# Hybrid GLA/MLA decoder layer on one core: the place of a head's block totals, and the order of accumulating transfers behind them

## The chip, the cores and the metric

The kernel runs on one core of a Trainium2 chip. The metric is the device time of one execution in microseconds; the time before is the median of three runs, 871.81 us (871.01 to 873.06). The engines have short names: PE (TensorE, with PEld for its weight loads), DVE (VectorE), ACT (ScalarE), POOL (GpSimd) and SP (SyncE). Each engine works through its own queue in order. Transfers are issued from the queue of an engine; in this kernel those that add into their destination are issued from POOL.

## The reference, cut to what matters

One layer on 512 tokens of width 1024, in float32. The normalised input goes through one wide input projection `w_in`, whose columns are split among a gated linear attention (GLA, four heads with 128 key and 256 value channels), a latent attention (MLA, eight heads) and two gates. Both branches are projected, gated, added and projected again; a squared-ReLU MLP follows. The part around the change is the GLA, for each head:

```
h = layer_norm(x);  q, k, v, r, a_lr, ... = split(h @ w_in)
log_a = log_sigmoid(a_lr @ w_gla_a2 + b_gla_a2) / 16
o_i = sum over j <= i of  (q_i * k_j * exp(sum of log_a over j+1..i)) . v_j
o   = rms_norm(o) * silu(r),  then @ w_o_gla
```

## The kernel before, in words

**The large products.** `w_in` is read in column sections. Each section r, v, a and b (the GLA's r and v, and the two gates) is one call of `unit`: a 512x1024x1024 product by a Winograd-like scheme with seven products n = 0 to 6 instead of eight. Their right sides are `RPH = ("T1","11","22","T2","21","T3","T4")`. "11", "22" and "21" are quarters of the section. T1, T2, T3 and T4 are sums of quarters, and they are made by transfers: `r_load` loads a quarter, and `r_add` adds another quarter into the tile that is there, by a transfer from POOL with `accum_op=add` (L623). T1 is loaded by SP (L625) and added into ahead of its unit, in `r_begin`. T2 is T1 with another quarter added, T3 is "22" with one added, and T4 is T2 with one added, each in two halves. An add must wait until the tile's old content has been used (split, below) or loaded.

**Splits.** Each right side is split into a high part (ACT, L190) and the remainder (DVE, L191), as the products run in three passes (L791 to L793 and L797 to L799) on such parts. `pump` traces the splits a little ahead of their use.

**GLA levels.** `gla_levels(h)` makes the scores of head h within a 512-token sequence by levels s = 1, 2, 4, ..., 256: at level s, pairs of neighbouring blocks of s tokens are multiplied. For each level ACT packs the operands into M (`pack`, L902), PE multiplies (L937), DVE takes the block into the scores (L909) and lets the decay in k grow to the next level (`grow`, L884), for which it needs the decay of whole blocks. These block totals come from `totals(h)`: seven additions on POOL, each of half the length of the last (L859, from 256 elements to 4), then two exponentials on ACT, of the head's log decays (L862) and of the totals (L863). `products(h)` makes q times k for the diagonal on POOL (L867), its high part on ACT (L869) and the remainder on POOL (L870). For head 0 both are traced when its levels begin (L917), for every other head in the fifth level (s = 16) of the head in front of it (L931).

**Order of the work.** The levels of all heads are one generator, `lane_levels`; `unit` advances it, with others, by `tick`: after each of its products but the last, and in unit r also in the middle of products 0, 2, 4 and 6, in the later units in the middle of each. So in unit r the levels of head 0 are traced like this: s = 1 behind product 0, s = 2 behind product 1, s = 4 in the middle of product 2, s = 8 behind it, s = 16 behind product 3. `r_add` for T2 is traced in product 0, that for T3 in product 2, the one for T4 in product 3, and that for the T1 of the next unit (`r_begin`) in product 3 too.

What is traced is not yet what is queued. The tile framework plans the queues (`schedule_with_timeline_sim=True`): what is traced earlier has priority, but whatever its own model of the time holds ready goes first. `tc.issue_after(ins)` adds an edge of order alone: what the block traces on the engine of `ins` is queued behind `ins`, without a wait for its end. On the chip each engine then keeps to the queue that was planned.

Of the kernel before, what the change touches and what calls it, by code (L numbers as in the profile page):

```python
# [16 lines left out]
ALU = mybir.AluOpType  # L17
# [9 lines left out]
GH = 4  # L27
# [25 lines left out]
def tile_hybrid_block(ctx: ExitStack, tc: tile.TileContext, I, out, dbg=None):  # L53
# [19 lines left out]
    def A(shape, dt=F32, n="a"):  # L73
        tag, bufs = ("C", 8) if n in TAG_C else (n, TAG_W[n]) if n in TAG_W else ("A", 24)
        return pa.tile(shape, dt, tag=tag, bufs=bufs, name=nm(n))

    def B(shape, dt=F32, n="b"):
        return pb.tile(shape, dt, tag="B", name=nm(n))
# [11 lines left out]
    def PX(shape=(P, T), dt=F32, n="px"):  # L90
        return px.tile(list(shape), dt, tag="px", name=nm(n))

    def f(ap):
        return ap.bitcast(F32)
# [5 lines left out]
    gtt = nc.gpsimd.tensor_tensor  # L100
# [8 lines left out]
    def split(src, hi, lo, scale=None):  # L109
        if scale is None:  # L110
            act(hi, src, AF.Copy)
            return vtt(lo, src, f(hi), op=ALU.subtract)
        else:
            act(hi, src, AF.Copy, scale=scale)
            return stt(lo, src, scale, f(hi), op0=ALU.mult, op1=ALU.subtract)
# [29 lines left out]
    st = {"dma": 0, "spl": 0, "gates": ()}  # L145
# [470 lines left out]
    def r_load(sec, op, i, j, hf, add=False):  # L616
        w = I["w_in"].rearrange("(k p) n -> p k n", p=P)
        if not add:
            RW[sec, op, hf] = A([P, 2, T], F32, "rw")
        k0 = 4 * i + 2 * hf  # L620
        c0 = UCOL[sec] + j * T
        if add:
            nc.gpsimd.dma_start(RW[sec, op, hf], w[:, k0:k0 + 2, c0:c0 + T], accum_op=ALU.add)  # L623
        else:
            nc.sync.dma_start(RW[sec, op, hf], w[:, k0:k0 + 2, c0:c0 + T])  # L625

    def r_begin(sec):
        for hf in range(2):
            r_load(sec, "T1", 0, 1, hf)
        r_add(sec, "T1", "T1", 0, 0)  # L630

    def r_add(sec, dst, src, i, j):
        for hf in range(2):
            RW[sec, dst, hf] = RW[sec, src, hf]
            r_load(sec, dst, i, j, hf, add=True)

    KEPT = {}

# [72 lines left out]
    def unit(sec, nxt=None):  # L711
# [65 lines left out]
        for n in range(7):  # L777
            o = a if n in (1, 3, 5) else b
            for hf in range(2):
# [22 lines left out]
                if n == 0 and hf == 1:  # L802
                    r_add(sec, "T2", "T1", 1, 1)
                    if later:
                        fetch("S2")
                if n == 2 and hf == 1:
                    r_add(sec, "T3", "22", 0, 1)
                    if later:
                        fetch("S3")
# [39 lines left out]
    QKP = [None] * GH  # L849
# [3 lines left out]
    def totals(h):  # L853
        t = TOT[h] = B([P, T], F32, "tot")
        src, o, n = GL[h], 0, T // 2
        while n >= 4:
            a = src.rearrange("p (n two) -> p n two", two=2)
            src = t[:, o:o + n]
            gtt(src, a[:, :, 0], a[:, :, 1], op=ALU.add)  # L859
            o += n  # L860
            n //= 2
        act(GL[h], GL[h], AF.Exp, scale=1.0 / 16.0)  # L862
        act(t[:, :o], t[:, :o], AF.Exp, scale=1.0 / 16.0)  # L863

    def products(h, qk):
        pr = B([P, T], F32, "pr")
        gtt(pr, qk[:, 0, :], qk[:, 1, :], op=ALU.mult)  # L867
        QKP[h] = [B([P, T], F32R, "qkp") for _ in range(2)]
        act(QKP[h][0], pr, AF.Copy)  # L869
        gtt(QKP[h][1], pr, f(QKP[h][0]), op=ALU.subtract)  # L870

    def gla_levels(h):
        qk = QK[h]
        QK[h] = None
        SD = B([P, NT, P], F32, "SD")
        s128 = kq = None

        def view(t, off, side, blk, step, s):
            return bass.AP(tensor=t.tensor, offset=t.offset + off, ap=[t.ap[0], [side, 2], [blk, T // (2 * s)], [step, s]])

        def grow(s):
            new = view(qk[:, 0, :], 0, T + s, 2 * s, 1, s)
            tot, o = (GL[h], 0) if s == 1 else (TOT[h], T - 2 * T // s)
            vtt(new, new, view(tot, o + 1, -1, 2, 0, s), op=ALU.mult)  # L884

        def half_lr(t2, s, i):
            v = t2[:, 0, :]
            return bass.AP(tensor=v.tensor, offset=v.offset + 2 * i * P,
                           ap=[v.ap[0], [2 * s, P // s], [T + s, 2], [1, s]])

        def packed(M, s, i):
            v = M[:, i, 0, :]
            return bass.AP(tensor=v.tensor, offset=v.offset,
                           ap=[v.ap[0], [2 * s, P // s], [s + (-2 * P if i else 2 * P), 2], [1, s]])

        def taken(v, s, step):
            return bass.AP(tensor=v.tensor, offset=v.offset + s, ap=[v.ap[0], [step, 2], [2 * s, P // s], [1, s]])

        def pack(s):
            M = B([P, 2, 2, P], F32, "M")  # L900
            for i in range(2):
                act(packed(M, s, i), half_lr(qk, s, i), AF.Copy)  # L902
            return M

        def take(s, p):
            nonlocal s128, kq
            if s <= 64:
                mk = lmask[:, LEVELS.index(s)].rearrange("p o u (n s) -> p o (u n) s", s=s)
                nc.vector.copy_predicated(taken(SD[:, 0, :], s, 2 * P - s), mk, taken(p[:, :2 * P], s, -s))  # L909
            elif s == 128:  # L910
                s128 = B([P, 2, 2, P], F32R, "s128")
                split(p[:, :256].rearrange("p (a b) -> p a b", b=P), s128[:, 0], s128[:, 1])
            else:
                split(p[:, :256], kq[:, 0, 0], kq[:, 0, 1])


        if h == 0:  # L917
            totals(0)
            products(0, qk)
        vtt(qk[:, 1, :], qk[:, 1, :], GL[h], op=ALU.mult)  # L920
        s = 1
        M = pack(1)
        yield
        diag = PX()
        for w in range(2):
            mm(diag, ones, QKP[h][w], start=w == 0, stop=w == 1)
        prev = None
        while s < T:
            if s == 2:
                vtt(SD, diag.rearrange("p (t i) -> p t i", i=P), ident[:, None, :].to_broadcast([P, NT, P]), op=ALU.mult)  # L930
            if s == 16 and h + 1 < GH:  # L931
                totals(h + 1)
                products(h + 1, QK[h + 1])
            p = PX()
            if s <= 64:
                for u in range(2):
                    mm(p[:, u * P:(u + 1) * P], M[:, 0, u, :], M[:, 1, u, :], start=True, stop=True)  # L937
            elif s == 128:
                for i in range(2):
                    mm(p[:, i * P:(i + 1) * P], qk[:, 0, 2 * i * P:(2 * i + 1) * P],  # L940
                       qk[:, 1, (2 * i + 1) * P:(2 * i + 2) * P], start=True, stop=True)
            else:
                for j in range(2):
                    nc.tensor.transpose(p[:, j * P:(j + 1) * P], qk[:, 0, j * P:(j + 1) * P], ident)
                kq = A([P, 2, 2, 256], F32R, "kq")
                split(qk[:, 1, 256:], kq[:, 1, 0], kq[:, 1, 1])
            if prev is not None:
                take(*prev)
            prev = (s, p)
            if s < 256:  # L950
                grow(s)
            s *= 2
            if s <= 64:
                M = pack(s)
            yield
        sd = A([P, 2, NT, P], F32R, "sd")
        p = PX()
        for u in range(2):
            nc.tensor.transpose(p[:, u * P:(u + 1) * P], SD[:, 2 + u, :], ident)
        act(sd[:, 0, :2], SD[:, :2], AF.Copy)  # L960
        gtt(sd[:, 1, :2], SD[:, :2], f(sd[:, 0, :2]), op=ALU.subtract)
        take(*prev)
        yield
        pt = p[:, :2 * P].rearrange("p (u i) -> p u i", i=P)
        split(pt, sd[:, 0, 2:], sd[:, 1, 2:])
        SS[h] = (sd, s128, kq)
        if h != 2:
            yield
# [212 lines left out]
    def lane_levels():  # L1181
        for o in range(2):
            with tc.issue_after(last_in.ins):
                nc.vector.tensor_copy(lmask[:, :, o], lmi[:, o, :, None, :].to_broadcast([P, len(LEVELS), 2, 64]))
        for h in range(GH):
            yield from gla_levels(h)
            lv[h] = True
# [413 lines left out]
```

## Time and profile before

| what | value |
|---|---|
| median of three runs | 871.81 us (871.01 to 873.06) |
| the profiled execution's own time | 871.12 us |
| its span, first to last instruction | 869.3 us |
| PE busy | 850.9 us, 98% of the span |
| DVE, ACT, POOL busy | 630.1, 485.7, 189.4 us |
| mean granted TensorE clock | 0.995 |
| L623, adds into tiles of sections | 32, 39.7 us of POOL |

The prediction works against the profiled execution, as all durations are its own, and then moves to the median. Rows of a timeline read: start in us from the span's start, duration in us, engine, line, operation, output and inputs by the program's names, shapes, count; in brackets how long the engine stood idle in front of it, and what ended that. In a table of waits a row reads: who waits, for whom, microseconds in total, times, the longest. In a table of groups: line, engine, operation, names and shapes, count, busy microseconds, mean nanoseconds of one, idle time in front. Rows that begin with a stretch of time give for each engine its busy time in it, with the number of instructions, then the granted clock, the DMA share and the rate.

### The profile page before, as it was taken

The numbers are of one execution on the slowest core, as the hardware profiler recorded it, in microseconds if no ns is written. First come the engines' busy times: TensorE is split into PE (matmuls) and PEld (weight loads), VectorE is DVE, ScalarE is ACT, GpSimd is POOL, SyncE is SP. The second block draws the span as 40 slices with busy tenths as digits, with TensorE's granted clock in tenths as the row PEclk, the third lists the DMA queues.
The fourth block names the chain that finished last, engine by engine and source line by source line (L and its number), as shares of the span: only waits on it lengthen the run. The fifth ranks groups of instructions, "written<-read, shape, count | busy, mean of one in ns | idle before, by whom it ended". The sixth has DMA issues, their size and how long they took to land. (4 is left out here: it accounts for less than half of the span.)

```text
span 869.3 us, 12408 instructions
## 1 busy us (share of the span) xinstructions
PE 850.9 (98%) x4594; PEld 736.0 (85%) x4594; DVE 630.1 (72%) x1023; ACT 485.7 (56%) x830; POOL 189.4 (22%) x220
## 2 busy tenths in 40 slices
PE   8999998999999999999999999999999999999995
PEld 5988777889999989888888888988888888888884
DVE  7967978988776657567766888986567546854687
ACT  5367757757674635455555324485366446745662
POOL 2304651625222210000000021005301520331023
PEclk9999999999999999999999999999999999999998
DMA  7746899998997614123136355008922990497075
GB/s 239 220 122 225 238 294 258 296 312 219 292 252 178 206 35 125 31 55 104 49 142 215 129 156 209 1 1 252 260 69 49 290 220 23 86 315 180 1 193 97
DMA packets 80924, 144.19 MB, mean 166 GB/s; under 512 B 9153, under 2 KB 35188, under 8 KB 80864
## 3 DMA queue, kind: packets, MB, share of 16 engines
q1 hardware_dynamic: 56480, 87.63, 29.8%
q0 software_dynamic: 22464, 52.11, 27.9%
q10 hardware_dynamic: 1920, 3.66, 1.3%
q8 instruction: 36, 0.59, 0.3%
q14 instruction: 24, 0.20, 0.1%
HBM read 116.64 MB, written 12.58 MB: 149 GB/s over the span
## 5 line engine op out<-in xcount | busy, mean ns | idle before, releaser
L191 DVE TENSOR_TENSOR wlo<-wraw,whi 128x1024 fp32r<-128x1024 f32 (+3 forms) x82 | 91.6, 1118 | 91.3 <-ACT whi L190 91.0
L190 ACT ACTIVATE whi<-wraw 128x1024 fp32r<-128x1024 f32 (+3 forms) x82 | 78.6, 959 | 62.7 <-PE mm L242 31.7
L242 PE MATMUL mm<-h,whi 128*128 128x512 f32 x288 | 112.1, 389 | 0.0
L241 PE MATMUL mm<-h,whi 128*128 128x512 f32 x288 | 112.1, 390 | 0.0
L243 PE MATMUL mm<-h,wlo 128*128 128x512 f32 x288 | 107.2, 389 | 0.0
L1463 POOL DMA_DIRECT2D res<-ev x54 | 47.7, 995 | 237.9 <-ACT ev L1461 194.3
L623 POOL DMA_DIRECT2D rw<-in_w_in_dram x32 | 39.7, 1240 | 110.4 <-DVE wlo L191 43.0
L243 PEld LDWEIGHTS mm<-h,wlo 128*128 128x128 f32 x288 | 54.0, 188 | 11.3
L241 PEld LDWEIGHTS mm<-h,whi 128*128 128x128 f32 x288 | 54.1, 188 | 11.1
L242 PEld LDWEIGHTS mm<-h,whi 128*128 128x128 f32 x288 | 54.1, 188 | 11.1
L191 DVE TENSOR_TENSOR wlo<-rw,whi 128x1024 fp32r<-128x1024 f32 x32 | 40.7, 1271 | 16.0 <-ACT whi L190 15.7
L1528 ACT ACTIVATE relu<-mm 128x512 f32<-128x512 f32 x32 | 18.8, 595 | 57.2 <-PE mm L243 57.2
L190 ACT ACTIVATE whi<-rw 128x1024 fp32r<-128x1024 f32 x32 | 33.8, 1057 | 18.7 <-PE mm L792 10.3
L382 POOL TENSOR_TENSOR mv<-mv,mhalf 128x1 f32<-128x1 f32 x4 | 4.1, 1035 | 169.3 <-DVE mv L381 169.3
L190 ACT ACTIVATE xh<-wraw 128x1024 fp32r<-128x1024 f32 (+1 forms) x24 | 23.3, 979 | 26.5 <-PE mm L276 15.2
L791 PE MATMUL mm<-S,whi 128*128 128x256 f32 x128 | 36.3, 288 | 0.0
L792 PE MATMUL mm<-S,whi 128*128 128x256 f32 x128 | 35.7, 283 | 0.0
L793 PE MATMUL mm<-S,wlo 128*128 128x256 f32 x128 | 34.5, 285 | 0.0
L191 DVE TENSOR_TENSOR wlo<-wq,whi 128x1024 fp32r<-128x1024 f32 x15 | 18.3, 1223 | 20.4 <-ACT whi L190 20.4
L191 DVE TENSOR_TENSOR xl<-wraw,xh 128x1024 fp32r<-128x1024 f32 (+1 forms) x24 | 26.2, 1110 | 5.9 <-ACT xh L190 5.9
L902 ACT ACTIVATE M<-qk 128x256 f32<-128x256 f32 x56 | 23.9, 456 | 8.4 <-DVE qk L884 7.5
L1461 ACT ACTIVATE ev<-mm 128x512 f32<-128x512 f32 x20 | 11.9, 601 | 27.8 <-DMA res<-ev 19.3
(473 smaller groups left out, 2730.4 us busy)
## 6 DMA issues: line engine op xcount, KB each, us to landing
rw<-in_w_in_dram POOLq DMA_DIRECT2D x32, 512.0 KB, 8.0
wraw<-in_w_ff_dram SPq DMA_DIRECT2D x32, 512.0 KB, 8.1
wq<-in_w_ff_dram POOLq DMA_DIRECT2D x32, 512.0 KB, 9.7
res<-ev POOLq DMA_DIRECT2D x54, 256.0 KB, 8.4
wraw<-in_w_in_dram SPq DMA_DIRECT2D x24, 512.0 KB, 5.0
S<-S SPq DMA_DIRECT2D x24, 512.0 KB, 6.7
rw<-in_w_in_dram SPq DMA_DIRECT2D x16, 512.0 KB, 8.7
S<-s SPq DMA_DIRECT2D x8, 512.0 KB, 5.1
```

The costliest lines, as they stand in the source:

```text
L190: st["ins"] = act(hi[:, :nk, :n], raw[:, :nk, :n], AF.Copy)
L191: vtt(lo[:, :nk, :n], raw[:, :nk, :n], f(hi[:, :nk, :n]), op=ALU.subtract)
L241: mm(o, hi[:, c], xh, start=first, stop=False)
L242: mm(o, hi[:, c], xl, start=False, stop=False)
L243: mm(o, lo[:, c], xh, start=False, stop=last)
L623: nc.gpsimd.dma_start(RW[sec, op, hf], w[:, k0:k0 + 2, c0:c0 + T], accum_op=ALU.add)
L791: mm(d, hi[:, c], xh, start=opens and q % 2 == 0, stop=False, skip_group_check=True)
L792: mm(d, hi[:, c], xl, start=False, stop=False, skip_group_check=True)
L793: mm(d, lo[:, c], xh, start=False, stop=closes, skip_group_check=True)
L902: act(packed(M, s, i), half_lr(qk, s, i), AF.Copy)
L1463: nc.gpsimd.dma_start(res[tt + t][:, j * T:(j + 1) * T], e, accum_op=ALU.add)
L1528: act(r, ps, AF.Relu)
```

## The change

The totals and products of head h + 1 are traced in the second level (s = 2) of head h, not in the fifth (s = 16). The last instruction of `products`, the subtraction on POOL, is remembered; every accumulating transfer that `r_add` traces after it has an edge of order to it, so that it stands behind the most recent `products` in POOL's queue. In unit r the adds into T2 are traced after products of head 0, and the adds into T3, into the T1 of unit v and into T4 are now traced after those of head 1.

```diff
@@ r_add
         for hf in range(2):
             RW[sec, dst, hf] = RW[sec, src, hf]
-            r_load(sec, dst, i, j, hf, add=True)
+            with ExitStack() as behind:
+                if "pool" in st:
+                    behind.enter_context(tc.issue_after(st["pool"].ins))
+                r_load(sec, dst, i, j, hf, add=True)
@@ products
-        gtt(QKP[h][1], pr, f(QKP[h][0]), op=ALU.subtract)
+        st["pool"] = gtt(QKP[h][1], pr, f(QKP[h][0]), op=ALU.subtract)
@@ gla_levels
-            if s == 16 and h + 1 < GH:
+            if s == 2 and h + 1 < GH:
                 totals(h + 1)
                 products(h + 1, QK[h + 1])
```

## The prediction

> **What bounds the kernel now.** I read the head of the page first, then the table of who waited for whom with TensorE alone, then the timelines of PE, ACT and POOL around its longest entry.
>
> ```profile
> span 869.3 us, 12408 instructions
> ...
> PE 850.9 (98%) x4594; PEld 736.0 (85%) x4594; DVE 630.1 (72%) x1023; ACT 485.7 (56%) x830; POOL 189.4 (22%) x220
> ...
> PE px L937 <- ACT M L902: 3.2, 1, 3.2
> ```
>
> TensorE is busy for 98% of the span, so the end of the kernel moves only when TensorE works with fewer holes. The last line is the head of the table of its waits (who waits, for whom, microseconds in total, times, longest): its longest single wait in the whole span is 3.2 us, once, for the packed operand M of a GLA level. The timeline of PE shows where, and what it costs beyond the hole itself (start, duration, engine, line, operation).
>
> ```profile
> 126.19 0.60 PE L937 MATMUL px<-M 128*128 128x128 f32 x4
> ...
> 126.87 0.40 PE L797 MATMUL mm<-whi,s 128*128 128x512 f32 x1
> 127.10 0.39 PE L798 MATMUL mm<-wlo,s 128*128 128x512 f32 x1
> ...
> 129.15 0.39 PE L797 MATMUL mm<-whi,s 128*128 128x512 f32 x1
> 132.69 1.02 PE L937 MATMUL px<-M 128*128 128x128 f32 x4 [3.16 <-ACT M L902]
> ...
> 133.93 0.63 PE L799 MATMUL mm<-whi,s 128*128 128x512 f32 x1
> ...
> 136.44 0.40 PE L797 MATMUL mm<-xh,s 128*128 128x512 f32 x1
> ```
>
> Before the hole one 512-column matmul follows another at 0.23 us (126.87 to 127.10). The next one after 129.15 was due at 129.38 and came at 132.69: 3.31 us lost. Behind it a matmul takes 0.63 us instead of 0.39: the six from 133.93 to 136.44 took 2.51 us where six at 0.23 are 1.38, so 1.13 are lost, and of the 1.24 us from 132.69 to 133.93 the same ratio (2.51 to 1.38) loses 0.56. The slow clock costs 1.7 us, and the hole 5.0 us together. The next two timelines show its cause.
>
> ```profile
> 119.54 0.64 ACT L869 ACTIVATE qkp<-pr 128x512 fp32r<-128x512 f32 x1
> 120.06 1.07 ACT L190 ACTIVATE whi<-rw 128x1024 fp32r<-128x1024 f32 x1
> ...
> 121.96 0.73 ACT L902 ACTIVATE M<-qk 128x256 f32<-128x256 f32 x2
> 130.46 0.63 ACT L863 ACTIVATE tot<-tot 128x508 f32<-128x508 f32 x1 [7.77 <-POOL tot L859]
> ...
> 131.94 0.70 ACT L902 ACTIVATE M<-qk 128x256 f32<-128x256 f32 x2
> ```
>
> ACT stands 7.77 us for the block totals of head 1, which only head 1's levels need, much later. ACT works its queue in order, so a weight split and the M of 131.94 stand behind it, and TensorE behind that M.
>
> ```profile
> 89.06 1.24 POOL L623 DMA_DIRECT2D rw<-in_w_in_dram  x1 [8.37 <-DVE xl L191]
> ...
> 97.53 1.34 POOL L870 TENSOR_TENSOR qkp<-pr,qkp 128x512 fp32r<-128x512 f32 x1
> ...
> 105.08 1.23 POOL L623 DMA_DIRECT2D rw<-in_w_in_dram  x1
> 105.86 0.78 POOL L584 MEMSET krl<- 128x256 f32 x1
> ...
> 112.23 1.16 POOL L859 TENSOR_TENSOR tot<-g 128x256 f32<-128x256 f32 x1
> 113.35 1.73 POOL L867 TENSOR_TENSOR pr<-qk 128x512 f32<-128x512 f32 x1
> ...
> 124.93 1.20 POOL L623 DMA_DIRECT2D rw<-in_w_in_dram  x1 [5.29 <-DMA rw<-in_w_in_dram]
> ...
> 128.42 1.20 POOL L623 DMA_DIRECT2D rw<-in_w_in_dram  x1 [0.78 <-DMA rw<-in_w_in_dram]
> 129.19 1.23 POOL L859 TENSOR_TENSOR tot<-tot 128x16 f32<-128x16 f32 x3
> ```
>
> POOL started head 1's totals at 112.23 and ended them at 130.42, because accumulating transfers lie between them in its queue. Those of 124.93 and 128.42 waited for the plain load into the same tile: they are the two adds into T1 of unit v, the only ones here whose tile a plain load fills. The other adds, in the order of their tiles, are T2 of unit r (89.06 and one more), T3 (105.08 and one more) and T4.
>
> **The change, part by part.** Walking the ticks of unit r: the second level of head 0 is traced behind product 1, the fifth behind product 3. So totals(1) and products(1) move two products forward: ahead of the adds of T3, of v's T1 and of T4, which were all traced ahead of them.
>
> *The stall.* The v T1 adds now have an edge behind the last products instruction, and the totals, traced ahead of that, come first by priority. Their waits for loads until 124.9 and 128.3 then hold nobody: what POOL has next is the split of head 0's scores, at the end of its levels. Removed: 5.0 us.
>
> *The moved instructions.* They are the same ones, with no more DMAs; one head's share is a quarter of these rows:
>
> ```profile
> L859 POOL TENSOR_TENSOR tot<-tot 128x128 f32<-128x128 f32 (+5 forms) x24 | 16.6, 693 | 0.7
> L867 POOL TENSOR_TENSOR pr<-qk 128x512 f32<-128x512 f32 x4 | 7.1, 1779 | 0.0
> L870 POOL TENSOR_TENSOR qkp<-pr,qkp 128x512 fp32r<-128x512 f32 x4 | 6.5, 1616 | 0.0
> L859 POOL TENSOR_TENSOR tot<-g 128x256 f32<-128x256 f32 x4 | 6.4, 1594 | 0.0
> ...
> rw<-in_w_in_dram POOLq DMA_DIRECT2D x32, 512.0 KB, 8.0
> ...
> rw<-in_w_in_dram POOLq DMA_DIRECT2D x1, 512.0 KB, 10.2
> ```
>
> That is (16.6 + 7.1 + 6.5 + 6.4) / 4 = 9.2 us of POOL for a head. The last two rows are the time from issue to landing of an add, the median of all and the one issued between 111 and 115 us. The memset of 105.86 is traced ahead of the totals, so I let head 1's work begin at 106.6, in time in which POOL now only waits.
>
> *What is late next.* v T1's second add, 128.42 + 8.0, lands at 136.4. Without the hole TensorE comes to it after products 5 and 6 (24 matmuls each, 5.5 us) and half of product 0, at 126.87 + 11.0 + 2.8 = 140.7; its split takes 2.3 us, so 2.0 are left (at 10.2 us it is 0.2 late). I take nothing off.
>
> *T2 of unit r.* Its adds now stand behind products(0), whose last instruction ends at 97.53 + 1.34 = 98.9. The first moves from 89.06 to 98.9, ten us, and the second stays 1.2 us behind it. The first lands at 98.9 + 8.0 = 106.9, or 109.1 with 10.2 us.
>
> ```profile
> 107.48 1.08 ACT L190 ACTIVATE whi<-rw 128x1024 fp32r<-128x1024 f32 x1
> ...
> 114.12 0.39 PE L797 MATMUL mm<-whi,s 128*128 128x512 f32 x1
> ```
>
> ACT splits it at 107.48 and TensorE uses it at 114.12; the split takes 1.08 us on ACT and 1.2 on DVE (the row of 107.93 below), so even at 109.1 it is ready near 111.4. Cost 0; the cover is the 2.7 us that are left.
>
> *T3 of unit r.* From 106.6 the last products instruction ends between 112.0 (first totals, product, ACT's copy and the remainder, about 5.4 us) and 115.8 (all 9.2 us first). So the first T3 add goes from 105.08 to 112.0–115.8, and the second 1.2 behind it. It lands between 120.0 (8.0) and 126.0 (10.2). TensorE needs its low part at 127.10; less 1.2 on DVE and 1.07 on ACT, ACT must start by 124.7; now it starts at 120.06. At the near end it costs nothing. At the far end ACT stands until 126.0, and the M behind both splits, now done at 122.7, would be done near 128.9 for the level that TensorE has at 126.19: 2.7 us. In the middle (landing 122 to 123) it is covered, and I take 0.5.
>
> *DVE beside POOL.* The moved work now runs beside a full DVE:
>
> ```profile
> 105.00:110.00 5.00, 5.00 (x24) 4.13 (x22) 5.00 (x8) 5.00 (x10) 1.97 (x4) 1.00 0.72 160
> ...
> 107.93 1.21 DVE L191 TENSOR_TENSOR xl<-rw,xh 128x1024 fp32r<-128x1024 f32 x1
> ...
> 111.10 0.68 DVE L884 TENSOR_TENSOR qk<-qk,tot 128x512 f32<-128x512 f32 x1
> 113.05 0.88 DVE L884 TENSOR_TENSOR qk<-qk,tot 128x512 f32<-128x512 f32 x1
> ...
> 159.81 2.35 DVE L884 TENSOR_TENSOR qk<-qk,tot 128x512 f32<-128x512 f32 x1
> 163.59 2.63 DVE L191 TENSOR_TENSOR wlo<-wraw,whi 128x1024 fp32r<-128x1024 f32 x1
> ...
> 110.68 0.39 PE L798 MATMUL mm<-xl,s 128*128 128x512 f32 x1
> ```
>
> The first row is the table of windows (PE, PEld, DVE, ACT, POOL busy): DVE and ACT are busy for all 5 us. Beside head 1's totals the product of L884 took 0.88 for 0.68 alone; beside head 2's it took 2.35, and a split 2.63 for 1.21. So one head stretches DVE by between 0.2 and (1.67 + 1.42) = 3.1 us. The split of 107.93 ends at 109.14 and is used at 110.68, 1.5 us of cover: TensorE pays 0 to 1.6 us. Head 1's row is the same product of the same unit, so I stay near it: 0.5. From below: DVE at 112 to 117 is relieved of the same, which is worth nothing as TensorE doesn't wait there.
>
> The Trainium skill speaks against this place: "GPSIMD Engine Reference", section 8, says that GpSimd shares its SBUF interfaces with VectorE and contends with VectorE instructions that have two SBUF inputs. The trace bears it out unevenly, 0.88 and 2.35 us for the same instruction; by the rule alone the larger stretch would be taken, 1.6 instead of 0.5, and the sum would be −2.9.
>
> *Heads 2 and 3.* Their totals move two products forward in the units v and a. TensorE waits for nothing there now, so nothing is won, and adds behind them may come up to one head's 9.2 us later: I take 0, with up to 1 us either way in the range.
>
> Sum: −5.0 + 0.5 + 0.5 = −4.0 us. The profiled execution took 871.12 us (its span and 1.8 around it), which gives 867.1. The median of the three runs is 0.69 above it: **867.8 us**. What a measurement can tell from no change is about 0.2%, 1.74 us.
>
> **The rivals.** *Stretched DVE (gain given back).* The splits of 107.93 and three more two-input instructions until 112 each take 1.4 to 1.7 us longer, as beside head 2: about 6 us, less 1.5 of cover. TensorE waits 4.5 and the time is 871.3, no change. For it: DVE is full there and cannot catch up. Against it: 0.88 at 113.05. With smaller T3 delays added the same band is reached; together 0.17. This is also where the skill's rule on the shared interfaces would lead.
>
> *Head 1's copy stays late (slower).* The adds of T3 hang on the copy of the products on ACT, L869. In the trace that copy ran at 119.54, though its product was ready at 113.35 + 1.73 = 115.1: ACT, in order, had other work. If ACT, which is full from 105 to 110, gets to it no sooner than now, products(1) end at 120.2 + 1.6 = 121.8, the first T3 add lands at 129.8 to 132.0, and its low part is ready at 132.1 to 134.3 against 127.1. TensorE then stands 5.0 to 7.2 us, with about 1.7 for the clock: 6.7 to 8.9 instead of 5.0, so 873.5 to 875.7, middle 874.6. It decides from an issue of T3 near 117 on (landing past 125 to 127); slower than before it is from about 120. For it: the copy was 4.5 us late in the trace. Against it: it is now traced ahead of T2's split, so it comes ahead of it by priority. Chance 0.15.
>
> On a short wait the Trainium skill ("TensorE: Matmul & The Clock Gate", Part 1) has the array throttled only after an idle window of about 3.4 us. By that rule a rest of 2.7 us mostly keeps its clock; no row here shows a hole of that size.
>
> *It doesn't do what it says.* The edge binds the adds to the products only, and not to the small totals, which have waits of their own; an add that the planner thinks ready could slip between them again and ACT would stand as before: 871.8. Against it: the adds whose loads come late are now two products behind. Chance 0.05.
>
> **How the numbers follow.** The forecast (gain between 1.8 and 5.5 us) has 0.61, the stretched DVE with small delays 0.17, the unchanged wait 0.05, slower 0.16 with all other mishaps, other small changes 0.01. That gives faster 0.61, same 0.23, slower 0.16. The range begins at the whole gain with half a microsecond from heads 2 and 3 and the spread of the runs below their median (0.8): 871.8 − 5.0 − 1.3 = 865.5. It ends where the slower case begins, 873.5. The likeliest case alone has 866.3 to 870.0.
>
> **What would show it.** Right: in the timeline of ACT no wait for the totals between 120 and 131, in that of PE no hole at 129 to 133 and 0.23 us pitches through it; POOL's totals of head 1 in one piece before 116, and the two v T1 adds behind them. The T2 adds of unit r start near 99. DVE's instructions at 107 to 112 stay near 0.9 and 1.3 us. Wrong: TensorE waiting for a low part (L191) or an M between 108 and 130, a T3 add issued later than 117, or a granted clock under 1.00 in a new place.

## The result, and the profile after

The changed kernel takes 877.1 us (median of 20 runs, 875.65 to 880.35); the kernel before, on the same chip, 871.2 us (20 runs). The ratio is 1.0067, 95% interval 1.0055 to 1.0080: by the ratio slower by 5.8 us, where 4.0 less were forecast. The profiled execution took 876.68 us.

The head of its page (the span, then busy time by engine):

```profile
span 874.6 us, 12402 instructions
...
PE 852.9 (98%) x4594; PEld 736.9 (84%) x4594; DVE 629.7 (72%) x1023; ACT 486.1 (56%) x830; POOL 191.1 (22%) x220
```

The span is 5.3 us longer, 2.0 of it busy time on TensorE (matmuls that take longer under a slow clock, below) and the rest idle. Two timelines of PE show where. First the kernel before, at the end of unit r, at both halves of the first product of unit v, and at the first matmul of the latent attention's queries:

```profile
143.74 0.38 PE L944 MATMUL px<-ca,qk 128*128 128x128 f32 x2
...
145.00 0.71 PE L797 MATMUL mm<-whi,S 128*128 128x512 f32 x2
...
147.82 0.39 PE L797 MATMUL mm<-xh,S 128*128 128x512 f32 x1
...
292.11 0.40 PE L274 MATMUL mm<-whi,latT 128*128 128x256 f32 x2
```

Then the changed kernel (its lines stand three further down):

```profile
140.17 0.38 PE L947 MATMUL px<-ca,qk 128*128 128x128 f32 x2
140.39 0.38 PE L962 MATMUL px<-ca,SD 128*128 128x128 f32 x2
140.53 0.71 PE L929 MATMUL px<-qkp,ones 128*128 128x512 f32 x2
144.47 1.22 PE L940 MATMUL px<-M 128*128 128x128 f32 x4 [3.23 <-ACT M L905]
145.35 1.20 PE L800 MATMUL mm<-whi,S 128*128 128x512 f32 x2
...
147.50 0.63 PE L802 MATMUL mm<-whi,S 128*128 128x512 f32 x1
147.93 0.63 PE L801 MATMUL mm<-wlo,S 128*128 128x512 f32 x1
...
151.29 0.39 PE L800 MATMUL mm<-xh,S 128*128 128x512 f32 x1
...
297.54 0.40 PE L274 MATMUL mm<-whi,latT 128*128 128x256 f32 x2
```

At the end of unit r the change is 3.6 us ahead (140.17 against 143.74). The second half of unit v's first product starts 3.5 us behind (151.29 against 147.82): 7.0 us are lost between. There is a new hole of 3.23 us, and behind it matmuls 0.43 us apart instead of 0.23 until 150.92 (granted clock 0.50 from 145 to 151). By the query product another 2.0 are lost (5.4 behind), and this stays to the end (5.3). Unit v has no part in these 2.0: unit a starts at 191.49 against 188.00, still 3.5 behind. Behind that start TensorE waits twice for a low part (0.97 us at 200.91, 0.58 at 244.51; in the kernel before once, 0.3). The first of these low parts is late for two reasons. ACT stood 2.85 us for T1 of unit a until 193.24, and VectorE behind it; then two VectorE subtractions take 1.86 us each instead of 0.68, while POOL runs head 3's first sum and product from 196.61 (the timelines of DVE and, last, of PE):

```profile
195.81 3.72 DVE L112 TENSOR_TENSOR vl<-rg,vh 128x512 fp32r<-128x512 f32 x2
199.44 1.41 DVE L191 TENSOR_TENSOR wlo<-wraw,whi 128x1024 fp32r<-128x1024 f32 x1
...
200.91 0.38 PE L796 MATMUL mm<-h,wlo 128*128 128x256 f32 x1 [0.97 <-DVE wlo L191]
```

The timeline of ACT says who made the hole of 3.23 us:

```profile
111.77 0.63 ACT L866 ACTIVATE tot<-tot 128x508 f32<-128x508 f32 x1 [2.47 <-POOL tot L862]
...
142.81 1.06 ACT L190 ACTIVATE xh<-rw 128x1024 fp32r<-128x1024 f32 x1 [4.97 <-DMA rw<-in_w_in_dram]
143.77 0.65 ACT L905 ACTIVATE M<-qk 128x256 f32<-128x256 f32 x1
144.22 1.05 ACT L190 ACTIVATE whi<-rw 128x1024 fp32r<-128x1024 f32 x1
```

The wait of 7.77 us for head 1's totals has become one of 2.47, at 111, and no long hole of TensorE follows it. The new one, 4.97 us, is for the second half of unit v's T1. Behind that split ACT's queue holds the M that TensorE waits for, and then the split of the first half. POOL's timeline shows that the change does what it says:

```profile
97.49 2.47 POOL L623 DMA_DIRECT2D rw<-in_w_in_dram  x2
...
104.72 0.61 POOL L862 TENSOR_TENSOR tot<-g 128x256 f32<-128x256 f32 x1
...
107.53 4.21 POOL L862 TENSOR_TENSOR tot<-tot 128x128 f32<-128x128 f32 x6
111.69 1.74 POOL L873 TENSOR_TENSOR qkp<-pr,qkp 128x512 fp32r<-128x512 f32 x1
113.38 3.65 POOL L623 DMA_DIRECT2D rw<-in_w_in_dram  x3
...
127.11 1.20 POOL L623 DMA_DIRECT2D rw<-in_w_in_dram  x1 [6.35 <-DMA rw<-in_w_in_dram]
131.09 1.20 POOL L623 DMA_DIRECT2D rw<-in_w_in_dram  x1 [2.78 <-DMA rw<-in_w_in_dram]
```

Head 1's totals run in one piece from 104.72 to 111.7; T2's adds leave at 97.49, and T3's with the first of T4 at 113.38. But the two adds into v's T1 wait for their plain loads until 127.11 and 131.09, against 124.93 and 128.42 before, and the second lands at 142.7. SP issued these loads 1.7 and 1.4 us later than before (from 115.52 on, against 113.81), and the second of them took 14.5 us to land instead of 13.1.

### The profile page after: what moved, and what is told of

Read it like the earlier page. It is cut to its first block, busy times and chain, and to the rows that moved or that the text cites. A ratio compares the mean times of both kernels' runs of the same rounds, so it can differ in the third digit from the quotient of the medians.

```text
span 874.6 us, 12402 instructions
## 1 busy us (share of the span) xinstructions
PE 852.9 (98%) x4594; PEld 736.9 (84%) x4594; DVE 629.7 (72%) x1023; ACT 486.1 (56%) x830; POOL 191.1 (22%) x220
## 5 line engine op out<-in xcount | busy, mean ns | idle before, releaser
L796 PE MATMUL mm<-h,wlo 128*128 128x256 f32 x96 | 25.9, 285 | 1.6 <-DVE wlo L191 1.6
```

Source lines behind the costliest of these rows:

```text
L796: mm(d, lo[:, c], xh, start=False, stop=closes, skip_group_check=True)
```

## The experiments

**Theory A**: the edge holds T3's adds behind head 1's products, so that they join the transfers that already crowd the time from 113 on; v's T1 lands later and ACT stands for it. **Its rivals**: the moved POOL work itself costs (B), the adds and totals still block each other (C), the loss lies with the later heads (D, E, F below). Ratios are to the kernel before on the same chip, with 95% intervals. Diffs are against the changed kernel unless said.

**No edge at all.** The four lines of `ExitStack` and edge are taken out; the totals stay at s = 2.

> Totals and products in the second level, no edge on any accumulating transfer. Theory A (the edge pushes the two T3 adds of unit r from 105-110 us to 113.4 us, into the busiest time of the transfers, so that the T1 adds of unit v land at 142.7 and not at 138, and ACT stands for them): T3 adds back at 105-110, v's second T1 add lands by 139.5, ACT waits under 1 us for it, the hole of TensorE at 141-144 is gone and the one of 129-132 stays away; 866 to 869 us where before has 871, ratio 0.994 to 0.998. Theory B (the moved POOL work itself, beside DVE and ahead of ACT's queue, delays the splits, and the edge has little to do with it): the hole at 141 stays, 874 to 877 us, ratio 1.004 to 1.007. Theory C (the two adds that wait for loads get between the totals again): the hole of 129 is back, 871.

872.92 us, ratio 1.0028 (1.0017 to 1.0038). That lies in none of the expected bands: the edge makes more than half of the loss, and not all of it.

**The edge alone.**

```diff
-            if s == 2 and h + 1 < GH:
+            if s == 16 and h + 1 < GH:
```

> Totals and products in the fifth level as before, the edges kept: only the T2 adds of unit r are later (behind the products of head 0, 97 us), and the totals of head 1 still have adds between them. Theory A: T2 late costs nothing; the hole at 129-132 stays, none at 141; ratio 0.999 to 1.002. If late T2 adds were what hurts: ratio over 1.004, with ACT or TensorE waiting for T2 between 107 and 115 us.

870.42 us, ratio 0.9997 (0.9984 to 1.0009). With the totals at the old place the edge costs nothing, though T2's adds leave late in it, too. So the edge costs only together with early totals.

**The edge, but not on T3.**

```diff
-                if "pool" in st:
+                if "pool" in st and dst != "T3":
```

> As after the change, but with the adds into T3 alone free of the edge (T2, T1 and T4 keep it). Theory A: the T3 adds go back to 105-110 us, which is enough: no hole at 141, 866 to 869 us, ratio 0.994 to 0.998, the same within 1 us as without any edge. Theory B: still 874 to 877, ratio 1.004 to 1.007.

872.81 us, ratio 1.0028 (1.0015 to 1.0041): the same as with no edge. What the edge costs is its hold on T3.

**The totals at s = 8**, behind product 2, where T3's adds are already traced.

> Totals and products in the fourth level (s = 8), traced behind the T3 adds and ahead of the T1 adds of the next unit; edges as after the change. Theory A: T3 adds free at 105-110, totals of head 1 before v's T1 adds: neither hole; 865 to 868 us, ratio 0.993 to 0.997. Theory B (POOL work beside a full DVE is what hurts): also better than after, since the work goes back to about 110-118 us, ratio 0.996 to 1.000. This run tells little between A and B alone; it is the version that either would choose.

871.89 us, ratio 1.0017 (1.0006 to 1.0028). T3 is not held here (its adds leave at 103.90 and 108.50), but those of T4 are, and still there is no gain: in its profiled execution, the fastest of this kernel (868.74), ACT stands 4.50 us for T4 at 130.25 and 3.70 us for v's T1 at 138.43.

**T3 of unit r cut to a quarter.** The two transfers carry 128 of their 512 columns.

```diff
-            nc.gpsimd.dma_start(RW[sec, op, hf], w[:, k0:k0 + 2, c0:c0 + T], accum_op=ALU.add)
+            n = T // 4 if (sec, op) == ("r", "T3") else T
+            nc.gpsimd.dma_start(RW[sec, op, hf][:, :, :n], w[:, k0:k0 + 2, c0:c0 + n], accum_op=ALU.add)
```

> As after the change, in the same queue places, but the two T3 adds of unit r move a quarter of their columns (128 of 512; three quarters of that sum are left out, so the output is another). Theory A2 (the T3 adds hurt by their bytes: pushed to 113.4 us, they share the transfer engines with the plain loads into v's T1, which then land late): those loads land 1 to 3 us sooner than at 127.1 and 131.0, v's second T1 add lands under 141, ACT's wait for it falls from 5.0 to 3 or less, and product 0 of unit v reaches its second half before 149 us instead of at 151.3; ratio 1.002 to 1.005. Rival (only the queue place counts: POOL or SP stands in order, and ACT's 2.5 us wait for head 1's totals delays SP): nothing moves, second half of product 0 at 151 +- 0.7, ratio 1.006 to 1.008.

872.71 us, ratio 1.0021 (1.0011 to 1.0031). That looks like proof that those bytes, coming late, delay T1. It is none: the control at the end of this section shows that the same cut helps the kernel before by as much.

**Head 1 alone at s = 2, no edge on T3.** Heads 2 and 3 go back to s = 16.

```diff
-                if "pool" in st:
+                if "pool" in st and dst != "T3":
...
-            if s == 2 and h + 1 < GH:
+            if s == (2 if h == 0 else 16) and h + 1 < GH:
```

> Head 1's totals and products alone in the second level (those of heads 2 and 3 in the fifth, as before), edges on all adds but T3. Theory D (head 3's totals beside DVE in unit a cost 2 us there, a cost of its own): from the first product of unit a to the first of the query product 103.4 to 103.8 us as before, not 105.5; ratio 0.996 to 1.000 where the same with all heads moved had 1.0028. Rival (the time before unit a is what sets unit a, by late transfers): unit a still takes about 105.5 us and the ratio stays at 1.002 to 1.003.

868.75 us, ratio 0.9973 (0.9962 to 0.9984): faster than both kernels, 2.4 us less than before.

**Head 3 alone at s = 2**, with all edges.

> Head 3's totals and products alone in the second level, those of heads 1 and 2 in the fifth, all edges kept. Theory D: units r and v as with the edge alone (hole at 129-132, unit a begins near 187.5), and units a and b take about 105.5 us instead of 103.4; a hole of TensorE for a low part near 195-200; ratio 1.001 to 1.003. Rival: units a and b take 103.4 to 103.8, ratio 0.999 to 1.001.

870.48 us, ratio 1.0000 (0.9989 to 1.0011). Theory D, that head 3's totals beside unit a's VectorE work make the rest of the loss, is not borne out by head 3 alone; the kernel with heads 1 and 3 below says more.

**Head 1 alone at s = 8**, with all edges.

> Head 1's totals and products alone in the fourth level, heads 2 and 3 in the fifth, all edges kept: the T3 adds stay free and the adds into v's T1 are behind the totals. Theory A: hole of 129-132 gone; what is left is ACT's wait for v's T1 add of about 1 to 4 us near 138; ratio 0.997 to 1.001. Were the transfers not what limits unit v's start, TensorE would keep the whole 5 us: ratio 0.994.

871.44 us, ratio 1.0006 (0.9993 to 1.0019). ACT stands 3.93 us for v's T1 at 140.52.

**Head 1 alone at s = 2 with every edge**: the pair that isolates T3.

```diff
-            if s == 2 and h + 1 < GH:
+            if s == (2 if h == 0 else 16) and h + 1 < GH:
```

> Head 1 alone moves to the second level, heads 2 and 3 stay at the fifth; the edge is on all accumulating transfers, T3's of unit r too. Theory A (the edge holds unit r's T3 adds behind head 1's products into the crowded transfers, and unit v's T1 lands late): slower than head 1 alone without that edge (0.9973) by about 4 us, so 1.000 to 1.003. Rival (the edge on T3 costs nothing, as the pair of the changed kernel with and without it, 1.0067 and 1.0028, would then differ by heads 2 and 3): 0.997, within 0.0015.

874.33 us, ratio 1.0038 (1.0026 to 1.0051). Against the same kernel without T3's edge that is 0.65%, 5.7 us, for the place of two transfers; bytes and instructions are the same. That the place of T3's adds costs this time is shown by the pair. The table of windows (PE, PEld, DVE, ACT, POOL busy, granted clock, DMA share, rate) has one row that tells them apart. With the edge:

```profile
110.00:115.00 5.00, 5.00 (x32) 4.19 (x31) 3.40 (x5) 3.27 (x6) 4.92 (x6) 1.00 0.33 115
```

Without it on T3:

```profile
110.00:115.00 5.00, 4.69 (x28) 3.73 (x26) 4.75 (x4) 0.99 (x3) 5.00 (x6) 1.00 1.03 283
```

While the edge holds T3's adds, the DMA engines are two thirds idle; then these and the first add of T4 start together, just ahead of the plain loads of T1. SP issued these loads from 115.03 on with the edge and from 115.66 on without it, so SP is not the cause. They took 10.7 and 14.2 us to land with the edge, 8.8 and 10.0 without it (tables of issues). POOL's timeline with the edge shows the adds that follow them (the last two rows, the first and the second add into T1; only the second waited for its load alone):

```profile
112.88 3.68 POOL L623 DMA_DIRECT2D rw<-in_w_in_dram  x3
...
126.24 1.20 POOL L623 DMA_DIRECT2D rw<-in_w_in_dram  x1 [5.98 <-PE px L940]
130.25 1.19 POOL L623 DMA_DIRECT2D rw<-in_w_in_dram  x1 [2.81 <-DMA rw<-in_w_in_dram]
```

and without it on T3, whose first add leaves here ahead of the totals:

```profile
104.02 1.19 POOL L623 DMA_DIRECT2D rw<-in_w_in_dram  x1
...
124.98 1.20 POOL L623 DMA_DIRECT2D rw<-in_w_in_dram  x1 [3.10 <-PE mm L802]
126.70 1.20 POOL L623 DMA_DIRECT2D rw<-in_w_in_dram  x1 [0.52 <-DMA rw<-in_w_in_dram]
```

The second add leaves 3.6 us earlier. ACT gets it 3.5 us earlier; with the edge:

```profile
142.44 1.06 ACT L190 ACTIVATE xh<-rw 128x1024 fp32r<-128x1024 f32 x1 [4.98 <-DMA rw<-in_w_in_dram]
```

without it on T3:

```profile
138.95 1.06 ACT L190 ACTIVATE xh<-rw 128x1024 fp32r<-128x1024 f32 x1 [1.06 <-DMA rw<-in_w_in_dram]
```

The wait of 4.98 us is that of the changed kernel (4.97) again, with heads 2 and 3 left alone. The Trainium skill ("DMA: Bandwidth & Descriptors", Queues, rings and completion order) says that each DMA engine takes turns between the queues that it has work for, packet by packet. The trace agrees so far as plain loads issued at nearly the same time take up to 4 us longer beside the adds (14.2 us against 10.0); it doesn't show the turns themselves.

**Only the exponential moves.** The kernel before, with ACT's exponential of the totals issued at the head's own start.

```diff
-        act(t[:, :o], t[:, :o], AF.Exp, scale=1.0 / 16.0)
+        if h == 0:
+            act(t[:, :o], t[:, :o], AF.Exp, scale=1.0 / 16.0)
@@ gla_levels
         if h == 0:
             totals(0)
             products(0, qk)
+        else:
+            with tc.issue_after(st["ins"].ins):
+                act(TOT[h][:, :508], TOT[h][:, :508], AF.Exp, scale=1.0 / 16.0)
```

> The kernel before, in which only one ScalarE instruction moves for heads 1 to 3: the exponential of the totals is issued at the head's own start, behind the splits then traced, so that no pack of the head before stands behind GpSimd's totals; GpSimd's own order stays. Theory A (the hole of 3.2 us at 129 and the slow clock behind it come from that one wait, and what can be won is cut by the landing of unit v's T1 at 138.3): no hole at 129, ratio 0.996 to 0.999. Rival B (the gain of head 1 alone comes from GpSimd's work and transfers leaving earlier): 1.000, within 0.001, with the time lost again ahead of unit v.

867.74 us, ratio 0.9971 (0.9958 to 0.9984). POOL and the transfers keep their old order, and the hole at 129 is gone. PE starts unit v at 140.20 (145.00 before), and ACT waits for v's T1 even so:

```profile
137.66 1.06 ACT L190 ACTIVATE xh<-rw 128x1024 fp32r<-128x1024 f32 x1 [1.77 <-DMA rw<-in_w_in_dram]
```

So the prediction's term for the stall is right by itself as far as the start of unit v (4.8 us of its 5.0), and T1's landing is next in line, close behind: at the second half of that product 3.7 us are left (144.17 against 147.82). The profiled executions differ by 4.1 us of span (865.2 to 869.3); over all runs the ratio is worth 2.5.

**Which of the later heads costs.** Three kernels without T3's edge move head 2 alone, heads 1 and 3, and heads 1 and 2; the diff is that of head 1 alone with another choice of heads.

> Head 2's totals and products alone move to head 1's second level; those of heads 1 and 3 stay at the fifth; the accumulating transfers wait behind the products, except those of T3. Theory E (head 2 is the part of the moved heads that costs: the mechanism of head 1 comes back one unit later, unit v's accumulating transfers leave late and those of unit a's T1 land late): the ratio to before is 1.002 to 1.005, with a wait of the splits at the start of unit a. Rival (neither head costs by itself, the loss of the kernels that move all three is made by their sum): 1.000, within 0.0015.

873.29 us, ratio 1.0035 (1.0020 to 1.0049): this kernel is slower, but that is not shown to be head 2's work. Of its profiled 2.5 us at the query product (294.57 against 292.11), 1.6 were there when unit v began, with a hole of 4.08 us ahead of it instead of 3.16, and POOL starts head 2's totals only at 146.83. SP issued the second load of v's T1 2.2 us later than before in this kernel; why is open. Only 0.9 came after.

> Heads 1 and 3 move to the second level of their predecessors, head 2 stays at the fifth; the edge is on every accumulating transfer but T3's. Theory E (head 2 alone costs, head 3 nothing): as with head 1 alone, 0.9973, within 0.0015. Rival (head 3's totals beside unit a cost when unit v comes early, which the kernel with head 3 alone could not show): 0.999 to 1.002.

869.75 us, ratio 0.9989 (0.9980 to 0.9998). Neither of the expected bands holds it well: 0.0016 above head 1 alone, 1.4 us, though head 3 alone costs nothing. The traces place it. From the first matmul of unit a to the query product this kernel takes 104.97 us, with head 1 alone 103.57. TensorE waits twice there for a low part (0.9 us together, none with head 1 alone), and a VectorE split beside head 3's totals takes 2.92 us instead of 1.21. The changed kernel loses its last 2.0 us in the same stretch (106.05 against 104.11 before). With head 3 alone the stretch takes 104.04 us, though a split takes 2.69 there; why TensorE then pays nothing stays open.

> Heads 1 and 2 move to the second level of their predecessors, head 3 stays at the fifth; the edge is on every accumulating transfer but T3's. Theory F (head 2's products stand ahead of unit v's T3 on GpSimd, so that those transfers leave later and collide with unit a's T1, as head 1's did one unit earlier): slower than head 1 alone (0.9973) by about 3 us, ratio 1.000 to 1.002, with a wait of ScalarE for unit a's T1 of some 3 us ahead of unit a. Rival (the loss is made only where heads 2 and 3 both move, or is head 3's): 0.997 to 0.999, without that wait.

871.49 us, ratio 1.0018 (1.0005 to 1.0031): with head 1 already early, head 2 costs 0.45%, 3.9 us, in time as theory F has it. In the kernel that moves all three heads without T3's edge, POOL's timeline shows the same picture as in unit r, one unit later: unit v's T3 (the pair at 152.86) stands behind head 2's totals.

```profile
148.41 4.51 POOL L862 TENSOR_TENSOR tot<-tot 128x64 f32<-128x64 f32 x5
152.86 2.43 POOL L623 DMA_DIRECT2D rw<-in_w_in_dram  x2
```

In the kernel before, the same two adds stand ahead of head 2's totals:

```profile
152.60 1.19 POOL L623 DMA_DIRECT2D rw<-in_w_in_dram  x1 [6.20 <-DVE wlo L191]
154.30 1.20 POOL L623 DMA_DIRECT2D rw<-in_w_in_dram  x1 [0.51 <-DMA rw<-in_w_in_dram]
```

Counted from the start of unit v (145.00 there, 142.1 here), they left at 7.6 and 9.3 us, and now at 10.7 and about 12. TensorE has a hole at the start of unit a, but not for T1, as theory F had it. It is ended by another transfer (the timeline of PE, first all heads moved without T3's edge, then heads 1 and 2 alone):

```profile
187.54 0.39 PE L795 MATMUL mm<-S,whi 128*128 128x256 f32 x1 [2.14 <-DMA S<-S]
...
188.24 0.58 PE L795 MATMUL mm<-S,whi 128*128 128x256 f32 x1 [1.19 <-DMA S<-S]
```

S is a left operand of unit a's first product, kept in memory and fetched back by SP in two transfers. With heads 1 and 2 moved, SP issued the first at 173.64 and then stood 6.2 us for a store of unit r's results (`rd<-rg`) to land; the second fetch left at 180.2 and took 8.0 us. With head 1 alone both had left by 175.4. Another hole, of 0.89 us, ended just ahead, at 186.69, which the profile puts down to VectorE; the first fetch landed then, too (173.64 + 12.9). Behind both holes the granted clock was 0.53 to 0.50 from 188 to 191. ACT's wait for T1 was 1.81 us there, not some 3, and no hole of TensorE over 0.3 us follows from it. So head 2's cost is shown, and its way over T1 is not.

**Is it the bytes of v's T3?** Heads 1 and 2 at s = 2, and v's T3 transfers cut to a quarter.

> As the kernel with heads 1 and 2 at the second level, but unit v's two T3 transfers carry 128 of their 512 columns, so that three quarters of that sum are left out of the result; all instructions and their order stay. Theory F (it is the bytes of T3, late, that delay unit a's T1): the wait of ScalarE for unit a's T1 falls under 1 us, and the ratio falls by 2 to 3 us against the kernel with whole transfers, to 0.997 to 0.999. Rival (GpSimd's and VectorE's time, or the place of the transfers, costs, not their bytes): the same ratio as with whole transfers, within 0.0012, and the wait stays.

868.28 us, ratio 0.9977 (0.9967 to 0.9987): 3.6 us come back, as theory F expects of the time. ACT's wait for T1 did not fall under 1 us as expected: it is 2.21 us at 185.85, against 1.81 at 187.31 with whole transfers. What changed is the fetch of S: the stores `rd<-rg` took 9.0 and 9.9 us to land instead of 13.6 (median of two), SP issued the second fetch at 174.6 instead of 180.2, and TensorE has no hole there.

**Two controls**: the same cuts where the adds are not held.

> Control: only head 1 moves (no edge on T3), and unit v's two T3 transfers carry 128 of their 512 columns, so that three quarters of that sum are left out of the result. Theory F (the bytes cost only where head 2's products hold those transfers back): no gain over head 1 alone, ratio 0.9973, within 0.0015. Rival (fewer bytes help any kernel here, so that the cut transfers in the kernel with heads 1 and 2 proved nothing): about 3 us less than head 1 alone, 0.993 to 0.995.

868.87 us, ratio 0.9981 (0.9971 to 0.9991): no gain over head 1 alone (0.9973). The bytes of v's T3 cost time with head 2 early and none without it. That it is their lateness, and not only that unit a then has no slack left for any transfer, is argued: no run here moves these two adds alone.

> Control: the kernel before, unit r's two T3 transfers carrying 128 of their 512 columns, so that three quarters of that sum are left out of the result; nothing else is changed. Theory A (those bytes cost only where the edge holds them back): 1.000, within 0.0015, the hole at 129 stays. Rival (fewer bytes there help any kernel, since unit v's T1 waits for its place among the transfers): GpSimd's wait for the base loads shrinks, the totals end earlier, and the ratio is 0.995 to 0.998.

866.71 us, ratio 0.9952 (0.9939 to 0.9965): here the rival is right. In unit r fewer bytes help the kernel before by 4.2 us, as much as they helped the changed one (1.0067 to 1.0021), so that pair proves nothing of lateness. The timelines of POOL and then of ACT show why:

```profile
121.47 1.20 POOL L624 DMA_DIRECT2D rw<-in_w_in_dram  x1 [1.48 <-DMA rw<-in_w_in_dram]
...
125.13 1.20 POOL L624 DMA_DIRECT2D rw<-in_w_in_dram  x1
```

```profile
127.16 0.63 ACT L864 ACTIVATE tot<-tot 128x508 f32<-128x508 f32 x1 [4.13 <-POOL tot L860]
```

The adds into T1 leave 3.3 to 3.5 us earlier than before (124.93, 128.42), as the plain loads under them land earlier, the totals end earlier, ACT stands 4.13 us instead of 7.77, and TensorE has no hole. The old stall, too, was made by when T1's loads land.

## Why the prediction was wrong

*The stall* (5.0 us off) held: no hole at 129, and 3.6 us ahead at the end of unit r, where the sum had said 4.0. The kernel with the exponential alone starts unit v 4.8 us ahead without the rest.

*T2 of unit r* at 0 held: its adds left at 97.49, and the edge without the early totals has the ratio 0.9997.

*T3 of unit r* at 0.5: the first add was issued at 113.38, inside the 112.0 to 115.8, and TensorE's waits between 110 and 120 are 0.41 and 0.36 us. As a delay of T3's own use the term was right, in part by luck: ACT stood 3.16 us for T3's second half, until 125.72, near the far end that was priced at 2.7, and TensorE paid nothing for it. But the step counted two transfers only for whom they serve, not for what they push.

*What is late next* is the step that failed: "v T1's second add, 128.42 + 8.0, lands at 136.4", and "I take nothing off". Three things were wrong in it. The issue: 131.09, not 128.42. SP issued the plain load under it 1.4 us later, and that load took 1.4 longer to land (14.5 against 13.1) once T3's adds had moved into its time. The duration: 8.0 us is the median over all units, and this very add took 10.2 in the kernel before, the case that the prediction had as 0.2 late. The issue table limited to 100 to 140 us, the kernel before, has

```profile
rw<-in_w_in_dram POOLq DMA_DIRECT2D x6, 512.0 KB, 9.8
...
rw<-in_w_in_dram SPq DMA_DIRECT2D x4, 512.0 KB, 13.7
```

and the changed kernel

```profile
rw<-in_w_in_dram POOLq DMA_DIRECT2D x6, 512.0 KB, 11.6
...
rw<-in_w_in_dram SPq DMA_DIRECT2D x4, 512.0 KB, 15.5
```

and 11.6 is also what this add itself took, so 131.09 + 11.6 = 142.7. And the need: 140.7 was when TensorE comes to the second half, but ACT splits the second half ahead of the M and of the first half (the rows 142.81 to 144.22), so that landing was needed soon after 137.8, where ACT began to stand. (For TensorE itself the sum was early: in the trace before it came to the second half at 147.82, which less 5.0 is 142.8; the sum left out the matmuls of the GLA in between.) Even the old issue with its own 10.2 us (138.6) had no slack; the exponential alone ran into that, with 1.77 us. The 4.97 us of ACT became 3.23 of TensorE, and with the slow clock behind it 7.0.

*Heads 2 and 3* at 0 ± 1 failed. The changed kernel loses nothing in unit v, and 2.0 us behind the start of unit a, where T1 of unit a (behind head 2's work) and VectorE beside head 3's totals are both late; no run parts the two in that kernel. The pair with head 1 (0.9973 to 1.0018) prices head 2 at 3.9 us where unit v comes early. Single prices don't add up (−2.4 for head 1, +5.7 for T3's edge, +3.9 for head 2 make 7.2 without head 3, not 5.8): in the changed kernel, where unit v comes late, TensorE has no hole for S at the start of unit a.

*DVE beside POOL* at 0.5: the splits beside head 1's totals took 1.51 and 1.42 us instead of 1.21, and TensorE waited for none, so for head 1 the term was nearer 0. But the step priced one head in one place. Beside head 3 the stretch, 0.68 to 1.86 us, is part of TensorE's wait of 0.97 at 200.91.

*The rivals.* The slower case was given 0.15 by head 1's copy; that copy ran at 108.33, not at 119.54, and T3 was issued ahead of 117. The slow case came true by another way, which the list of rivals had not: a transfer that lands late for the next unit. The stretched DVE, given 0.17, has its share in that wait, but for head 3 in unit a and not for head 1. Of the signs listed as wrong, a granted clock under 1.00 in a new place appeared, at 145 to 151, and a wait for an M between 108 and 130 only as the 0.36 us at 119.14.

## What to carry to other kernels

Where several tiles are filled by transfers in one stretch, moving one transfer later can move the landing of the transfers issued beside it: before adding an edge of order, look at the DMA share by windows, and don't hold a ready transfer while the DMA engines would be idle. Price a landing with transfers of the same stretch, not with the median of the whole run, and ask what stands behind the waiting instruction in its queue, not only when its own result is needed. Before you name the transfer that made a hole, read which one ended it. A stall made by one early wait in an ordered queue may be cured by moving that one instruction: here the exponential alone (0.9971) does what the early totals of head 1 do (0.9973) and leaves POOL and the transfers in their old order.

## What the hardware showed that was not expected

Short holes are not always cheap. After the hole of 2.14 us at the start of unit a (the kernel with all heads, no edge on T3) the table of windows has

```profile
186.00:188.00 2.00, 0.46 (x3) 0.46 (x4) 0.47 (x1) 0.57 (x1) 0.11 (x1) 1.00 1.06 405
188.00:190.00 2.00, 2.00 (x13) 2.00 (x12) 1.48 (x3) 2.00 (x6) 0.00 (x0) 0.55 1.07 382
190.00:192.00 2.00, 2.00 (x12) 2.00 (x12) 2.00 (x3) 0.17 (x2) 1.95 (x3) 0.60 1.08 288
```

a granted clock of 0.55 and 0.60 over four microseconds, where the hole of 1.14 us at the same place in the kernel with head 2 alone kept 1.00. Two holes close together, of 0.89 and 1.19 us, were followed by 0.53 (heads 1 and 2). These are one execution each. The prediction cited the Trainium skill ("TensorE: Matmul & The Clock Gate", Part 1) for an idle window of about 3.4 us ahead of a throttle; here a hole of 2.14 us was followed by one, and the measurement decides.

The stretch of VectorE beside POOL is large and uneven. The two subtractions of 128x512 in the row of 195.81 took 3.72 us together while POOL worked for head 3; in the kernel before they took 0.68 each (at 190.08 and 191.01), which is 2.7 times less. Beside head 1's totals a split took at most 1.51 us for 1.21.
